# Seven block products in another order, and the work beside the heads planned anew: a hybrid recurrent layer on one core

## The chip, the cores and the metric

The kernel runs on one core of one Trainium2 chip. The metric is the device time of one execution in microseconds; for the kernel before it is the median of three runs.

## The reference, cut to what matters

One layer on 1024 tokens of width 1024, all in float32. The part that the change touches is the mixing layer: one wide projection of the normalised input, two recurrent branches, and their gates.

```
h = rmsnorm(x)
proj = h @ w_in               # q,k,v,z of 8 delta heads; q,k,v,r of 4 GLA heads; two merge gates
q_a, k_a, v_a = silu(conv4(...))          # branch A: gated delta rule, chunks of 64, 8 heads of 128
o_a = rmsnorm(gated_delta_rule(...)) * silu(z)
o_b = rmsnorm(gla(q_b, k_b, v_b, gate)) * silu(r)     # branch B: 4 heads, values of 256
merged = sigmoid(gate_a) * (o_a @ w_a) + sigmoid(gate_b) * (o_b @ w_b)
x = x + merged @ w_out
x = x + cross_attention(rmsnorm(x), rmsnorm(mem))
x = x + relu(rmsnorm(x) @ w1) ** 2 @ w2
return rmsnorm(x)
```

## The kernel before, in words

Float32 products are made of three TensorE passes (`mm3`, lines 584, 586 and 588): both operands are split into a rounded high part and a low remainder, and high by high, high by low and low by high are added in one PSUM tile. ScalarE makes the high part of a weight block (line 624, or 986 where the block is negated), VectorE the low part (625, 987).

The large projections are computed by a seven-product scheme for 2x2 blocks. A **unit** is one such projection of 256 columns. The seven products p0 to p6 take a sum of weight blocks A11, A12, A21, A22 and a fixed sum of input blocks each. In the trace the input block names the product: A0a is p0, A0b is p1, t2, t4 and t6 are p2, p4 and p6 (all three read "t" in the profile), A1b is p3 and A1a is p5. Each product is 12 matmuls of 512 columns. The products of a unit add into three PSUM banks (`BANK`): p0, p2, p4 and p6 all add to the first, p1 has the second alone, p3 and p5 share the third. After each product its bank is read once: p0, p3 and p2 are copied out by ScalarE (line 937), p1, p4 and p5 are added to the result by VectorE (942 to 946), p6 goes to an activation. The next product of the same bank adds to what stands there, so its first matmul waits until the bank has been read.

In the phase with the GLA heads (`phase_gla`, some 150 to 707 us in the profile) the weight sums are not formed by an engine. `gla_w` lets GpSimd issue four accumulating transfers per unit (line 972, `more`), each of which adds a 256 KB block from HBM to a block in SBUF. In a unit's program order they are: the **first sum** A21 += A22, at p0; the **second sum** A11 += A21, behind p0's split, used by p4; the **third sum** A21 += A11, behind p3's split, used by p2; the **fourth sum** A21 += A12, behind p2's split, used by p5. So p3 must come before p2 and p2 before p5. The split weights lie in a ring of four buffers ("wop", `RING`), the raw blocks in four ("raw"), which is two units.

The units of one GLA head are r, then k, q and v of two delta heads, then qk of the next GLA head. Beside them run the GLA head's own work (gates, scores, a scan of eight steps, norm, output), the short convolution (line 1316) and, in `phase_gdn` (some 707 to 1110 us), the delta heads: a forward substitution on VectorE (`gdn_subst`), an inverse by TensorE (lines 1490 and 1499), a scan per pair of heads, and dense units beside it (gates 5 to 15, z, and the folded attention weights Q and O).

Two things set the order of instructions. The program pushes the dense units as generators on a queue and takes a number of matmuls from it at each place (`fill`, with the constants FA to FJ, SFILL, PFILL, TFILL, and the lists EXTRA, FILL and LASTG). Then a planner (`Plan`) replays the traced program with a cost for each instruction and fixes the order on every engine; each engine runs its list in order. LAYP and LAYQ set the places of the delta heads' buffers in SBUF.

Of the kernel before, what the change touches and what calls it, by code (L numbers as in the profile page):

```python
# [37 lines left out]
DIRP, FW = (6,), 5  # L38
DXB = 6
EXB, THB, GLOV, TE = 5, 1, (0, 2, 4, 6), 1  # L40
FA, FB, FC, FD, FE, FG, FH, FI = 23, 31, 30, 28, 47, 24, 0, 0
SE = ((0, 0, 0, 0, 0, 0, 0, 0), (0, 1, 0, 1, 1, 1, 0, 1), (0, 1, 0, 1, 0, 1, 0, 0))
FJ = 24
KRAW = 4
LAYW = (("raw", 2048, 2), ("whi", 4096, 2), ("wlo", 4096, 2))
FF = ((24, 24), (24, 24))
# [11 lines left out]
def bcol(t, n):  # L58
# [5 lines left out]
           "Reciprocal", "StreamTranspose", "TensorScalarAffineSelect")  # L64
ENGINES = {mybir.EngineType.PE: "tensor", mybir.EngineType.DVE: "vector", mybir.EngineType.Activation: "scalar",
           mybir.EngineType.Pool: "gpsimd", mybir.EngineType.SP: "sync"}
EXTRA = (('v', 'k', 't', 'q'), ('v', 't', 'k', 'q'), ('k', 'v', 't', 'q'), ('k', 'v', 't', 'q'))
QB, FOLDB = 2, 1
SFILL, PFILL, TFILL = 4, (2, 12), (4, 14, 0, 10, 10, 6)
FILL = ((7, 'z6'), ('z0', 6, 10, 'Q2'), (9, 'O1', 'z5', 'z3', 'Q3', 'z1'), ('z2', 'z4', 'O0', 11, 'O3', 'z7', 8, 'Q1', 5), ('O2', 13, 'Q0', 12))  # L70
LASTG = (14, 15)
LAYP = (('PF', 8192, 1), ('pr', 1024, 1), ('NT1', 4096, 2), ('NT0', 4096, 2), ('Pm', 4096, 1), ('dm', 4096, 2), ('k0', 4096, 2), ('kdt0', 4096, 2), ('kdt1', 4096, 2), ('k1', 4096, 2), ('q', 4096, 2))
LAYQ = (('AT', 4096, 2), ('v0', 4096, 2), ('X', 4096, 2), ('sz', 2048, 2), ('v1', 4096, 2), ('acc', 2048, 2))
OUT = "out_0_dram"
HOLD, MARGIN = 0, 0
SOON = 0
# [12 lines left out]
class Op:  # L89
# [7 lines left out]
    def __init__(self, ins, flex):  # L97
        eng = self.eng = ENGINES[ins.engine]
        ins_, outs = [[x for x in q if getattr(x, "bass_ap", None) is not None] for q in (ins.ins, ins.outs)]
        n = size(outs[0])  # L100
        psum = lambda x: x.bass_ap.tensor.name[:3] in ("pd_", "ps_")
        self.name, self.opcode, self.acc = ins.name, ins.opcode, []
        for w, q in enumerate((ins_, outs)):
            for x in q:
                p = x.ap[0][0]
                lows, span = [x.bass_ap.offset % p if p > 1 else x.bass_ap.offset], 0
                for st, k in sorted(x.ap[1:]):
                    if st <= span + 1 or k * len(lows) > 16:
# [12 lines left out]
        times = {"vector": (150 + scan + n * 1.042 + 60 * scalar, 85, 34, 35), "gpsimd": (290 + n * 1.98 if sums else 160 + n * 0.9, 45, 60, 35)}  # L121
        if sums and n <= 16:
            times["gpsimd"] = 430 + n * 152, 45, 60, 35
        if ins.opcode == "TensorReduce":
            times["vector"] = 420, 85, 34, 35
        if ins.opcode == "StreamTranspose":
            times["vector"] = 1880 if far else 1245, 85, 34, 35
        if ins.opcode == "Memset" and far:
            times["gpsimd"] = 450, 45, 60, 35
        self.times = {e: (d - early, early + own, early + lat) for e, (d, early, own, lat) in times.items()}  # L130
        if ins.opcode == "DMACopy":
            self.dma, self.cost, self.own, self.lat = True, ISSUE, LAND, LAND
            self.bytes = n * 4 * outs[0].ap[0][1]
            if eng == "gpsimd":
                self.cost, self.bytes = 1200, 2 * self.bytes
            if ins_[0].bass_ap.tensor.name in HEADIN:
                self.bytes *= RATE / 390
        elif eng == "tensor":
            m = size(ins_[0])
            if ins.is_transpose:  # L140
                self.cost = m * 0.85
            elif ins_[0].dtype == F32R:
                self.cost = m * 0.4463 + (4 if m < HALF else 0)
            elif max(m, size(ins_[1])) == 64:
# [358 lines left out]
class Layer:  # L503
# [454 lines left out]

        return evict

    SUMS = (0, 1, 3, 2, 4, 5, 6)

    def gla_w(self):
# [8 lines left out]
        more = lambda dst, src: nc.gpsimd.dma_start(dst, src, accum_op=ADD)  # L972

        for p in self.SUMS:
            for o, (a, src) in zip(ops, bl):
                A11, A12, A21, A22 = a
                if p == 0:
                    more(A21, src[3])
                if A11.shape[-1] == P:
                    t = self.til(wp, [P, 2, n, P], "wop", F32R, bufs=RING)  # L980
                    o[p] = t[:, 0], t[:, 1]
                else:
                    o[p] = [self.til(wp, [P, n, 256], "wop", F32R, bufs=RING) for _ in range(2)]
                w, (hi, lo) = (A11, A12, A21, A21, A11, A21, A22)[p], o[p]
                if p in (2, 3, 6):
                    nc.scalar.activation(hi, w, AF.Copy, scale=-1.0)  # L986
                    nc.vector.scalar_tensor_tensor(lo, w, -1.0, hi.bitcast(F32), MUL, SUB)  # L987
                else:
                    self.split(w, hi, lo, nc.vector if p in GLOV else None)
                if p in (0, 2, 3):  # L990
                    more(*{0: (A11, src[2]), 3: (A21, src[0]), 2: (A21, src[1])}[p])
        return n, ops

    def gla_dense(self, evicts, after=None):

        n, ws = self.gla_w()
        yield
        bank = self.banks(2)
        for p in self.SUMS:
            if p == 2:  # L1000
                self.fetch_w()
            for i, (w, evict) in enumerate(zip(ws, evicts)):
# [11 lines left out]
                pt, new = bank(p, i)  # L1014
# [1503 lines left out]
```

## Time and profile before

| | before |
|---|---|
| median of three runs | 2169.34 us (2164.31 to 2181.07) |
| profiled execution | 2169.7 us |
| its span | 2167.8 us |
| TensorE (PE) busy | 2112.3 us, 97% |
| VectorE (DVE) busy | 1540.3 us, 71% |
| ScalarE (ACT) busy | 1208.5 us, 56% |
| GpSimd (POOL) busy | 229.3 us, 11% |
| mean granted TensorE clock | 0.995 |

The profiled execution is 0.4 us above the median, and 1.9 us of it lie outside the span. TensorE is busy nearly all the time, so only the time in which it waits, or runs at a lower clock, can be won by another order. GpSimd's busy time counts the issue of a transfer and not its flight.

### The profile page before, as it was taken

Reading aid. Unit: us, or ns where it says so; the run is one execution under the profiler, and the core shown is the slowest. Engines: PE = TensorE matmul, PEld = TensorE weight load, DVE = VectorE, ACT = ScalarE, POOL = GpSimd, SP = SyncE. Lnnn points to the kernel's source line nnn. Section 1 sums busy time; section 2 is a strip of 40 time slices with the busy share of each in tenths; the row PEclk is TensorE's granted clock in tenths of the full one; section 3 lists DMA queues with packets and bytes.
Section 4 is the critical chain, followed back from the end, with each engine's and each line's share of the span. In section 5 each row is a group of like instructions: output and inputs, shape, how many; then the busy total and the mean of one; then the engine's idle time right before and its main releaser. Section 6 shows DMA issues by size and latency. Waiting matters only on the chain. (4 is left out here: it accounts for less than half of the span.)

```text
span 2167.8 us, 31186 instructions
## 1 busy us (share of the span) xinstructions
PE 2112.3 (97%) x10938; PEld 1784.9 (82%) x10938; DVE 1540.3 (71%) x2744; ACT 1208.5 (56%) x2393; POOL 229.3 (11%) x260
## 2 busy tenths in 40 slices
PE   8999989999899999999999999999999999999998
PEld 8888767798677889889988888888788888888787
DVE  7846857636656678869558899659968667566755
ACT  7456746635645657586645455665755557443433
POOL 0112111111111423121100000000100000000000
PEclk9999999999999999999999999999999999999999
DMA  8554554644545634544487762325454456778742
GB/s 321 153 126 91 131 123 98 162 102 99 155 94 142 209 97 161 185 151 161 147 284 231 235 222 80 114 88 166 129 177 133 151 174 203 249 248 273 239 158 102
DMA packets 171613, 355.81 MB, mean 164 GB/s; under 512 B 18488, under 2 KB 27192, under 8 KB 171456
## 3 DMA queue, kind: packets, MB, share of 16 engines
q1 hardware_dynamic: 158064, 327.57, 45.5%
q0 software_dynamic: 13248, 26.22, 7.7%
q8 instruction: 86, 1.41, 0.3%
q14 instruction: 71, 0.58, 0.1%
q10 hardware_dynamic: 144, 0.03, 0.0%
HBM read 253.57 MB, written 100.17 MB: 163 GB/s over the span
## 5 line engine op out<-in xcount | busy, mean ns | idle before, releaser
L624 ACT ACTIVATE wop<-raw 128x512 fp32r<-128x512 f32 (+1 forms) x451 | 291.5, 651 | 362.1 <-PE pd L588 157.5
L625 DVE TENSOR_TENSOR wop<-raw,wop 128x512 fp32r<-128x512 f32 (+1 forms) x428 | 298.9, 702 | 231.8 <-ACT wop L624 226.2
L584 PE MATMUL pd<-t,wop 128*128 128x512 f32 x332 | 133.6, 402 | 19.4 <-ACT wop L986 10.4
L588 PE MATMUL pd<-t,wop 128*128 128x512 f32 x332 | 132.1, 398 | 0.9 <-DVE wop L987 0.9
L586 PE MATMUL pd<-t,wop 128*128 128x512 f32 x332 | 131.6, 396 | 0.0
L584 PE MATMUL pd<-A1b,wop 128*128 128x512 f32 x272 | 106.4, 392 | 0.0
L586 PE MATMUL pd<-A1b,wop 128*128 128x512 f32 x272 | 106.1, 390 | 0.0
L588 PE MATMUL pd<-A1b,wop 128*128 128x512 f32 x260 | 101.3, 391 | 1.6 <-DVE wop L987 1.6
L584 PEld LDWEIGHTS pd<-t,wop 128*128 128x128 f32 x332 | 63.2, 190 | 41.2 <-ACT wop L986 13.3
L1316 DVE SCALAR_TENSOR_TENSOR dx<-dx,convw,dx 128x1023 f32<-128x1023 f32 (+2 forms) x72 | 91.0, 1288 | 7.5 <-ACT dx L1314 6.8
L987 DVE SCALAR_TENSOR_TENSOR wop<-raw,wop 128x512 fp32r<-128x512 f32 (+1 forms) x69 | 50.8, 736 | 58.3 <-ACT wop L986 58.1
L986 ACT ACTIVATE wop<-raw 128x512 fp32r<-128x512 f32 (+1 forms) x69 | 45.8, 664 | 79.3 <-PE pd L588 29.9
L584 PE MATMUL pd<-A1a,wop 128*128 128x512 f32 x208 | 82.0, 394 | 3.7 <-ACT wop L624 3.5
L586 PE MATMUL pd<-A1a,wop 128*128 128x512 f32 x208 | 81.1, 390 | 0.0
L588 PEld LDWEIGHTS pd<-t,wop 128*128 128x128 f32 x332 | 63.4, 191 | 16.7 <-DVE wop L987 3.4
L588 PE MATMUL pd<-A1a,wop 128*128 128x512 f32 x196 | 76.9, 393 | 0.0
L586 PEld LDWEIGHTS pd<-t,wop 128*128 128x128 f32 x332 | 63.2, 190 | 12.4
L624 ACT ACTIVATE whi<-raw 128x512 fp32r<-128x512 f32 x70 | 43.2, 628 | 41.6 <-PE pd L586 28.1
L584 PEld LDWEIGHTS pd<-A1b,wop 128*128 128x128 f32 x272 | 51.1, 188 | 10.6 <-ACT wop L624 0.3
L586 PEld LDWEIGHTS pd<-A1b,wop 128*128 128x128 f32 x272 | 51.1, 188 | 10.3
L588 PEld LDWEIGHTS pd<-A1b,wop 128*128 128x128 f32 x260 | 48.8, 188 | 12.0 <-DVE wop L987 2.0
L625 DVE TENSOR_TENSOR wlo<-raw,whi 128x512 fp32r<-128x512 f32 x64 | 43.6, 685 | 16.1 <-ACT whi L624 15.8
(654 smaller groups left out, 6587.9 us busy)
## 6 DMA issues: line engine op xcount, KB each, us to landing
raw<-in_w_dram SPq DMA_DIRECT2D x120, 256.0 KB, 4.1
raw<-in_w_dram SPq DMA_DIRECT2D x32, 512.0 KB, 3.8
e<-ad SPq DMA_DIRECT2D x63, 256.0 KB, 4.8
ad<-q SPq DMA_DIRECT2D x45, 256.0 KB, 2.8
rawa<-ad SPq DMA_DIRECT2D x42, 256.0 KB, 4.6
A0b<-tgd SPq DMA_DIRECT2D x32, 256.0 KB, 4.5
ad<-acc SPq DMA_DIRECT2D x30, 256.0 KB, 2.3
ad<-u SPq DMA_DIRECT2D x30, 256.0 KB, 2.8
```

Source lines behind the costliest of these rows:

```text
L584: nc.tensor.matmul(out, lh, rh, start=first and i == 0, stop=False, skip_group_check=True)
L586: nc.tensor.matmul(out, lh, rl, start=False, stop=False, skip_group_check=True)
L588: nc.tensor.matmul(out, ll, rh, start=False, stop=last and i == n - 1, skip_group_check=True)
L624: nc.scalar.activation(hi, raw, AF.Copy)
L625: (lo_eng or nc.gpsimd).tensor_tensor(lo, raw, hi.bitcast(F32), SUB)
L986: nc.scalar.activation(hi, w, AF.Copy, scale=-1.0)
L987: nc.vector.scalar_tensor_tensor(lo, w, -1.0, hi.bitcast(F32), MUL, SUB)
L1316: self.nc.vector.scalar_tensor_tensor(y[:, d:], x[:, :T - d], cw[:, 3 - d:4 - d], y[:, d:], MUL, ADD)
```

## The change

The seven products of a unit get one of two orders. Units with one result tile set run p0, p3, p2, p1, p4, p5, p6, so that two neighbours never add to the same PSUM bank. The first unit (two evictions) and the two v units of the GLA heads (a list of two) keep the order of before, p0, p1, p3, p2, p4, p5, p6. The next unit's raw blocks are fetched at the fourth product, as before. The accumulating transfers stay, with their program order in `gla_w` following the products.

Beside that the numbers that place the work change: fewer matmuls are taken behind the scores (FC) and behind the next gate (FD), one at each step of the GLA scan (FH, none before), EXTRA puts k first in the first head and v first in the other three, the dense units of the delta heads are dealt out in another way (gate 14 comes in earlier and gate 5 later), and two SBUF layouts are permuted. The planner takes 900 ns, not 1200, for GpSimd's issue of a transfer.

```
-FA, FB, FC, FD, FE, FG, FH, FI = 23, 31, 30, 28, 47, 24, 0, 0
+FA, FB, FC, FD, FE, FG, FH, FI = 23, 31, 22, 20, 46, 24, 1, 0
-FJ = 24
+FJ = 12
-EXTRA = (('v', 'k', 't', 'q'), ('v', 't', 'k', 'q'), ('k', 'v', 't', 'q'), ('k', 'v', 't', 'q'))
+EXTRA = (('k', 'v', 't', 'q'), ('v', 't', 'k', 'q'), ('v', 't', 'k', 'q'), ('v', 't', 'k', 'q'))
-SFILL, PFILL, TFILL = 4, (2, 12), (4, 14, 0, 10, 10, 6)
+SFILL, PFILL, TFILL = 3, (6, 12), (4, 14, 0, 8, 14, 10)
-FILL = ((7, 'z6'), ('z0', 6, 10, 'Q2'), ...
+FILL = ((7,), ('z0', 6, 10, 'z6', 'Q2'), ...
-LASTG = (14, 15)
+LASTG = (15, 5)
...
-                self.cost, self.bytes = 1200, 2 * self.bytes
+                self.cost, self.bytes = 900, 2 * self.bytes
...
-    SUMS = (0, 1, 3, 2, 4, 5, 6)
+    SUMS = ((0, 3, 2, 1, 4, 5, 6), (0, 1, 3, 2, 4, 5, 6))
...
-        for p in self.SUMS:
+        for p in order:
...
-        n, ws = self.gla_w()
+        order = self.SUMS[len(evicts) > 1 or isinstance(evicts[0], list)]
+        n, ws = self.gla_w(order)
...
-        for p in self.SUMS:
-            if p == 2:
+        for i, p in enumerate(order):
+            if i == 3:
                 self.fetch_w()
```

What the planner makes of it is shown at three places. First TensorE, at the second delta unit of the first head (k before, v after): the first matmul of each of its seven products. pd names the PSUM tile, the next name is the input block. Before:

```order
L584 MATMUL pd_330_2514<-A0a_10_202,wop_323_2490 128x512
L584 MATMUL pd_332_2529<-A0b_11_203,wop_324_2494 128x512
L584 MATMUL pd_333_2543<-A1b_163_1270,wop_325_2497 128x512
L584 MATMUL pd_330_2514<-t2_152_1157,wop_326_2501 128x512
L584 MATMUL pd_330_2514<-t4_153_1158,wop_327_2505 128x512
L584 MATMUL pd_333_2543<-A1a_12_204,wop_328_2508 128x512
L584 MATMUL pd_330_2514<-t6_154_1159,wop_329_2511 128x512
```

The same engine and place in the change:

```order
L584 MATMUL pd_330_2518<-A0a_10_202,wop_323_2494 128x512
L584 MATMUL pd_332_2533<-A1b_163_1270,wop_324_2498 128x512
L584 MATMUL pd_330_2518<-t2_152_1157,wop_325_2502 128x512
L584 MATMUL pd_336_2565<-A0b_11_203,wop_326_2506 128x512
L584 MATMUL pd_330_2518<-t4_153_1158,wop_327_2509 128x512
L584 MATMUL pd_332_2533<-A1a_12_204,wop_328_2512 128x512
L584 MATMUL pd_330_2518<-t6_154_1159,wop_329_2515 128x512
```

p2 (t2) moved from the fourth to the third place, one product sooner, and p1 (A0b) now stands between p2 and p4 (t4), which add to one bank.

Second GpSimd's list, where the qk unit of the second head follows the q unit: the sums of qk and the first sum of the r unit behind it. Before:

```order
L972 DMA raw_355_2729<-in_w_lqk_dram 128x512 [waits DVE_49]
L972 DMA raw_369_2870<-in_w_lr_dram 128x512 [waits DMAHW1_49,DMASW4_49,DMASW1_49]
L972 DMA raw_355_2729<-in_w_lqk_dram 128x512 [waits DMASW3_49,DVE_49]
L972 DMA raw_355_2729<-in_w_lqk_dram 128x512 [waits DMASW7_49,DVE_49]
L972 DMA raw_369_2870<-in_w_lr_dram 128x512 [waits DVE_49]
```

In the change:

```order
L972 DMA raw_354_2728<-in_w_lqk_dram 128x512 [waits DVE_49]
L972 DMA raw_354_2728<-in_w_lqk_dram 128x512 [waits DMASW3_49,DVE_49]
L972 DMA raw_368_2869<-in_w_lr_dram 128x512 [waits DMAHW0_49,DMASW4_49,DMASW1_49]
L972 DMA raw_354_2728<-in_w_lqk_dram 128x512 [waits DMASW6_49,DVE_49]
L972 DMA raw_368_2869<-in_w_lr_dram 128x512 [waits DVE_49]
```

The first row is qk's second sum, and the row that waits for a hardware transfer (DMAHW) is r's first sum. It stood between qk's second and third sums and stands now between the third and the fourth.

Third ScalarE's list at the same second delta unit. L937 copies p0's bank out, L986 makes p2's high part. Before:

```order
L1314 ACTIVATE dx_322_2482<-dx_318_2417,convw_6_194 128x1024
L937 ACTIVATE dx_331_2527<-pd_330_2514 128x512
L1084 ACT_TABLE_LOAD
L1084 ACTIVATE dx_321_2462<-dx_321_2462 128x512
L986 ACTIVATE wop_326_2501<-raw_319_2419 128x512
L624 ACTIVATE wop_327_2505<-raw_319_2419 128x512
```

In the change:

```order
L1078 ACTIVATE dx_317_2403<-pd_308_2338 128x512
L1315 ACTIVATE dx_322_2484<-dx_317_2403,convw_6_194 128x1024
L986 ACTIVATE wop_325_2502<-raw_318_2418 128x512
L624 ACTIVATE wop_326_2506<-raw_319_2419 128x512
L937 ACTIVATE dx_331_2531<-pd_330_2518 128x512
```

The copy of p0's bank stood ahead of p2's split and stands now behind it and behind p1's split.

More of the change, by code (lines that the diff above doesn't have):

```diff
@@ L66 @@
            mybir.EngineType.Pool: "gpsimd", mybir.EngineType.SP: "sync"}
-EXTRA = (('v', 'k', 't', 'q'), ('v', 't', 'k', 'q'), ('k', 'v', 't', 'q'), ('k', 'v', 't', 'q'))
+EXTRA = (('k', 'v', 't', 'q'), ('v', 't', 'k', 'q'), ('v', 't', 'k', 'q'), ('v', 't', 'k', 'q'))
 QB, FOLDB = 2, 1
-SFILL, PFILL, TFILL = 4, (2, 12), (4, 14, 0, 10, 10, 6)
-FILL = ((7, 'z6'), ('z0', 6, 10, 'Q2'), (9, 'O1', 'z5', 'z3', 'Q3', 'z1'), ('z2', 'z4', 'O0', 11, 'O3', 'z7', 8, 'Q1', 5), ('O2', 13, 'Q0', 12))
-LASTG = (14, 15)
-LAYP = (('PF', 8192, 1), ('pr', 1024, 1), ('NT1', 4096, 2), ('NT0', 4096, 2), ('Pm', 4096, 1), ('dm', 4096, 2), ('k0', 4096, 2), ('kdt0', 4096, 2), ('kdt1', 4096, 2), ('k1', 4096, 2), ('q', 4096, 2))
-LAYQ = (('AT', 4096, 2), ('v0', 4096, 2), ('X', 4096, 2), ('sz', 2048, 2), ('v1', 4096, 2), ('acc', 2048, 2))
+SFILL, PFILL, TFILL = 3, (6, 12), (4, 14, 0, 8, 14, 10)
+FILL = ((7,), ('z0', 6, 10, 'z6', 'Q2'), (9, 14, 'O1', 'z5', 'z1'), ('z2', 'z4', 'z3', 'O0', 11, 13, 'O3', 'Q0', 'Q1'), ('Q3', 'z7', 'O2', 12, 8))
+LASTG = (15, 5)
+LAYP = (('PF', 8192, 1), ('k1', 4096, 2), ('NT1', 4096, 2), ('NT0', 4096, 2), ('Pm', 4096, 1), ('dm', 4096, 2), ('k0', 4096, 2), ('kdt0', 4096, 2), ('kdt1', 4096, 2), ('pr', 1024, 1), ('q', 4096, 2))
+LAYQ = (('AT', 4096, 2), ('v0', 4096, 2), ('acc', 2048, 2), ('sz', 2048, 2), ('v1', 4096, 2), ('X', 4096, 2))
 OUT = "out_0_dram"
@@ L959, in joined, with gla_w @@
         return evict
-    SUMS = (0, 1, 3, 2, 4, 5, 6)
-    def gla_w(self):
+    SUMS = ((0, 3, 2, 1, 4, 5, 6), (0, 1, 3, 2, 4, 5, 6))
+    def gla_w(self, order):
         nc, wp = self.nc, self.wp
@@ L994, in gla_dense @@
     def gla_dense(self, evicts, after=None):
-        n, ws = self.gla_w()
+        order = self.SUMS[len(evicts) > 1 or isinstance(evicts[0], list)]
+        n, ws = self.gla_w(order)
         yield
         bank = self.banks(2)
-        for p in self.SUMS:
-            if p == 2:
+        for i, p in enumerate(order):
+            if i == 3:
                 self.fetch_w()
-            for i, (w, evict) in enumerate(zip(ws, evicts)):
+            for u, (w, evict) in enumerate(zip(ws, evicts)):
                 x, (hi, lo) = self.bs[p], w[p]
@@ L1013, in gla_dense @@
                     continue
-                pt, new = bank(p, i)
+                pt, new = bank(p, u)
                 yield from self.mm3(pt, [((hi[:, k], lo[:, k]), (x[:, 0, k], x[:, 1, k])) for k in range(n)], new, p in (1, 5, 6))
```

## The prediction

> **What bounds the kernel now.** The page's first part is read first: who is busy, and for how much of the span.
>
> ```profile
> PE 2112.3 (97%) x10938; PEld 1784.9 (82%) x10938; DVE 1540.3 (71%) x2744; ACT 1208.5 (56%) x2393; POOL 229.3 (11%) x260
> ```
>
> TensorE (PE) is busy for 2112.3 of 2167.8 us. The change removes no matmul, so at most the other 55.5 us, and what is lost to a lower clock, can be won. Next comes the table of busy time by stretches: the phase with the GLA heads, the delta heads, and what follows (length, then busy time with count of PE, PEld, DVE, ACT and POOL, the granted clock, the DMA share, GB/s).
>
> ```profile
> 150.00:707.00 557.00, 524.64 (x2766) 434.44 (x2765) 362.53 (x511) 306.13 (x494) 91.94 (x108) 0.99 0.50 119
> 707.00:1110.00 403.00, 398.17 (x2644) 355.86 (x2642) 305.63 (x756) 260.71 (x750) 93.78 (x115) 0.99 0.50 165
> 1110.00:2167.80 1057.80, 1045.76 (x4684) 865.36 (x4682) 769.59 (x1321) 557.09 (x1007) 28.28 (x18) 1.00 0.55 181
> ```
>
> PE stands idle for 557.00 - 524.64 = 32.4 us in the GLA phase, 4.8 in the delta phase and 12.0 in all that follows, which is twice as long. The GLA phase is where the change works. What it waits for there, in the table of waits (waiting line, what it waited for, us in total, times, longest):
>
> ```profile
> PE pd L584 <- ACT wop L986: 10.9, 7, 2.9
> PE pd L584 <- ACT dx L937: 6.6, 9, 2.2
> PE pd L584 <- ACT wop L624: 4.9, 6, 1.3
> PE pd L588 <- DVE wop L987: 2.4, 2, 1.6
> PE pd L584 <- ACT qk L937: 2.1, 3, 0.7
> PE pd L586 <- DVE wop L625: 1.1, 1, 1.1
> PE pd L586 <- DVE wop L987: 1.0, 2, 0.8
> PE pd L584 <- DVE qk L946: 0.5, 1, 0.5
> ```
>
> There are two families. L937 and L946 read a bank out: PE waits to add to a bank that the product before it has just filled. These **bank waits** are 6.6 + 2.1 + 0.5 = 9.2 us in 13 places. The others wait for split weights (**weight waits**): 10.9 + 2.4 + 1.0 = 14.3 us on L986 and L987 (the negated blocks of p3 and p2, mostly p2's, which needs the third sum) and 4.9 + 1.1 = 6.0 on L624 and L625; 20.3 together.
>
> **The bank waits.** One of them from near, on PE's timeline (start, us, instruction, idle before it and what ended it), at p2 and then p4:
>
> ```profile
> 385.33 0.39 PE L586 MATMUL pd<-t,wop 128*128 128x512 f32 x1
> 385.55 0.39 PE L588 MATMUL pd<-t,wop 128*128 128x512 f32 x1
> 386.63 0.50 PE L584 MATMUL pd<-t,wop 128*128 128x512 f32 x1 [0.69 <-ACT dx L937]
> ```
>
> Matmuls start every 0.22 to 0.23 us, so a product of 12 takes 2.7 us. The first of p4 starts 1.08 us after the last of p2, 0.85 more than the pace, where the idle column says 0.69. The thirteen places cost 9.2 + 13 x 0.16 = 11.3 us. With p1 between p2 and p4 the copy has 2.7 us to happen in, and needs this:
>
> ```profile
> L937 ACT ACTIVATE dx<-pd x51: 576/598/604, 107.5 to 694.4; 128x512 f32<-128x512 f32 x51
> ```
>
> 0.6 us. So the waits behind p2 go whole, -11.3, unless ScalarE's list puts the copy late. It does that elsewhere: the order of the change shows p0's copy behind p2's split, and p2 adds to p0's bank. By the whole list that is so in 7 of 20 units, against 3 before. There p2's first matmul waits for the split, which it needs anyway, then for p1's split and the copy, each about 0.6 us: 1.2 us, but only where the third sum comes late. I take three such cases, 3 x 1.1 = +3.3. **Bank waits: -8** (bounds -11.3 and -11.3 + 7 x 1.2 = -3).
>
> **The weight waits.** For a sum one reads GpSimd's rows beside those of the engines that use it. At the second q unit (p3's split; then on GpSimd its second sum, a foreign first sum of qk, its third sum; then p2's split and p2's first matmul):
>
> ```profile
> 556.22 0.69 DVE L987 SCALAR_TENSOR_TENSOR wop<-raw,wop 128x512 fp32r<-128x512 f32 x1
> ...
> 553.13 0.89 POOL L972 DMA_DIRECT2D raw<-in_w_gq_dram  x1 [8.05 <-DVE wop L625]
> 558.55 0.88 POOL L972 DMA_DIRECT2D raw<-in_w_lqk_dram  x1 [4.53 <-issue]
> 562.64 0.88 POOL L972 DMA_DIRECT2D raw<-in_w_gq_dram  x1 [3.22 <-DVE dx L1316]
> ...
> 566.90 0.63 ACT L986 ACTIVATE wop<-raw 128x512 fp32r<-128x512 f32 x1 [2.40 <-DMA raw<-in_w_gq_dram]
> ...
> 567.58 0.49 PE L584 MATMUL pd<-t,wop 128*128 128x512 f32 x1 [1.44 <-ACT wop L986]
> ```
>
> The split at 556.22 (p3's) released the third sum, but that was issued at 562.64, because the second sum was in flight from 553.13 and another unit's first sum stood between. One accumulating transfer follows another: the issues lie 5.42 and 4.09 us apart, as far as one takes to land.
>
> ```profile
> DMA to landing us min/median/max: 3.6/4.1/6.7
> ```
>
> So place in GpSimd's list decides, and a transfer costs its unit 4.1 us. In the change that foreign sum stands between the third and the fourth (the second place shown above) at this unit, and likewise at two others whose p2 waits are these:
>
> ```profile
> 298.00 0.50 PE L584 MATMUL pd<-t,wop 128*128 128x512 f32 x1 [2.87 <-ACT wop L986]
> 614.97 0.50 PE L584 MATMUL pd<-t,wop 128*128 128x512 f32 x1 [2.87 <-ACT wop L986]
> ```
>
> There the third sum comes 4.1 us sooner, and p2 is wanted 2.7 us sooner, so 1.4 us is won: 2.87 becomes 1.5 twice and 1.44 goes, -4.2. The fourth sum waits for p2's split, one product sooner before p5 than until now: 2.7 us, more than any of L624's six waits (longest 1.3), so their 4.9 go. Against that, p2 comes one product sooner in every unit that has the new order. Those that waited for L986 or L987 anyway would pay up to 2.7 us each: seven at most, 19 us. The lower bound is nothing, if the split before, now also a product sooner, brings its sum sooner. Since most units of before show no p2 wait I stay near nothing, at +2. **Weight waits: -7** (bounds -20.3 and -9 + 19 = +10).
>
> **The clock.** The stretches with a granted clock of 0.50:
>
> ```profile
> 299.70:303.10 3.40, 2.85 (x7) 1.66 (x6) 0.00 (x0) 0.81 (x2) 0.25 (x1) 0.50 0.90 207
> 381.60:385.00 3.40, 3.02 (x7) 2.46 (x8) 3.08 (x5) 1.61 (x2) 0.88 (x1) 0.50 0.87 286
> 569.40:572.80 3.40, 3.40 (x12) 2.81 (x11) 0.00 (x0) 2.12 (x5) 0.14 (x1) 0.50 0.72 152
> 787.80:794.60 6.80, 6.17 (x29) 6.18 (x30) 1.20 (x3) 5.52 (x10) 1.95 (x6) 0.50 0.25 77
> ```
>
> Each follows a wait: 2.87 us before 298.00, 1.44 before 567.58, a p2 wait at 380.39 and, in the delta phase, this:
>
> ```profile
> PE ps L1490 <- ACT PF L1478: 2.6, 1, 2.6
> PE ps L1542 <- ACT dl L1537: 0.9, 1, 0.9
> ```
>
> At half rate a stretch loses half its length: 3 x 1.7 + 3.4 = 8.5 us. The windows fall where waits happen to lie, so with fewer waits I take half: **-4** (bounds -8.5, and +7 should four more appear).
>
> The Trainium skill bears on this in "TensorE: Matmul & The Clock Gate", section "Part 1: The HAM clock gate (the "warmup" mystery)": it says that the clock drops to half after at least one idle window of about 3.4 us. The rows here disagree: the waits ahead of these stretches are 2.9 us and shorter, so the measurement decides. By the page's rule no wait of this kernel would cost clock, this term would be 0 and the sum 4 us less of a gain, 2154.
>
> **The delta phase and the rest.** Between the first gram products and the inverse at L1490 stands dense work that covers the substitution. Counted in the two lists at the pace of the rows above, it grows from 55 to about 59 us, which is past the 55 + 2.6 that the substitution took. But each scan step now gets three matmuls, not four (SFILL), so the 0.9 us wait may come back several times. Of 3.5 us I take **-1** (bounds -3.5 and, if each of the last scan's eight steps waits 0.9, +7). The planner's 900 ns and the layouts add no work; behind 1110 us the code is the same, and its largest wait is this:
>
> ```profile
> PE pd L584 <- ACT q L937: 1.7, 1, 1.7
> ```
>
> That stage gets 0.
>
> **Sum.** -8 - 7 - 4 - 1 = -20 us. Against the profiled execution's 2169.7 (span 2167.8 and 1.9 outside), that gives **2150**, 0.9% less. The profiled execution lies 0.4 us above the median of 2169.34, so no correction is made.
>
> **Rivals.** *All weight waits go too.* If the earlier place of p2's and p3's splits pulls the sums along, the terms are -11.3, -20.3, -8.5 and -3.5: -43.6, so **2126**. For it: the ring has a free buffer one product sooner. Against it: the sums follow each other at 4.1 us and more whatever the splits do.
>
> *The chain of sums takes the gain back.* A unit needs first, second and third sum in a row before p2, and that is as long as before while PE arrives 2.7 us sooner. Seven times 2.7 is +19, with -11.3 for the banks, -4 for the clock and the p5 waits partly back: about +3, **2172**. For it: the 2.40 us in which ScalarE waited for the sum at 566.90, so the chain is without slack there. Against it: most units show none.
>
> *Slower: a foreign first sum ahead of a unit's own second.* The third rival is told by these rows, of GpSimd and then PE:
>
> ```profile
> 361.08 0.88 POOL L972 DMA_DIRECT2D raw<-in_w_gq_dram  x1 [12.27 <-DMA raw<-in_w_gq_dram]
> 365.47 0.88 POOL L972 DMA_DIRECT2D raw<-in_w_gk_dram  x1 [3.51 <-DVE dx L944]
> ...
> 374.85 0.50 PE L588 MATMUL pd<-A1b,wop 128*128 128x512 f32 x1 [1.57 <-DVE wop L987]
> 380.39 0.50 PE L584 MATMUL pd<-t,wop 128*128 128x512 f32 x1 [1.20 <-ACT wop L986]
> ```
>
> At 361.08 GpSimd waited for q's raw block, 12.27 us, with k's second sum (365.47) queued behind; k's p3 and p2 waited afterwards. Before, the list has this at one k unit and one v unit. In the change it stands so at the second unit of each of four heads. If the raw block is late each time, the unit loses one transfer's landing and one sum, 4.1 + 4.4 = 8.5 us: 4 x 8.5 = 34, with four more halved windows +7, less the bank's 11.3: +30, **2199**. It decides as soon as the raw load lands later than p0's split. Against it: with 12.27 us of waiting, only 1.57 and 1.20 reached PE.
>
> That the change does nothing is excluded for the order: PE's rows above show p1 between p2 and p4.
>
> **How the numbers follow.** Forecast 0.48, all weight waits go 0.16, the chain takes it back 0.20, slower 0.16. The forecast's own range, with each term about half way to its bounds (4, 7, 6 and 3 us, which make 10 to 12 when added as squares), is 2138 to 2162. A change of under 1% (21.7 us, so 2148 to 2191) is about what a measurement of this kernel can't tell from none. Faster: 0.16 and some two fifths of the forecast's 0.48, 0.36. Slower: 0.16 and a little of the chain's case, 0.18. The rest, 0.46, is within 1%. The range must leave out no more than 0.2: from 2126, which leaves out half of the fastest case, to 2186, which leaves out most of the slowest.
>
> **What will show it.** In the GLA phase the waits of L584 for dx and qk of L937 should fall from 8.7 us to 2 to 4, all of them now at p2 and none at p4; L624's 4.9 should be gone; L986 and L987 should keep 9 to 13. There should be one or two halved windows, and L1490's wait under 1 us. The forecast is wrong if GpSimd's rows show waits for raw blocks ahead of a second sum that PE pays in full (slower), if p2 waits 2 us or more in over six units (no change), or if p2 waits nowhere (faster).

## The result: no difference, and the profile after

The changed kernel takes 2170.34 us, median of 20 runs; the kernel before takes 2167.34 us over 20 runs beside it. The ratio is 1.0013, 95% interval 1.0000 to 1.0026. The forecast was 2150 us, 0.9% faster. The time is inside the range given, but no gain came. The profiled execution after took 2173.8 us, with a span of 2172.1 us against 2167.8 before.

First the busy times on the page of the changed kernel, then its stretches (the same columns as before, same bounds):

```profile
PE 2115.9 (97%) x10938; PEld 1791.6 (82%) x10938; DVE 1543.5 (71%) x2740; ACT 1211.6 (56%) x2395; POOL 231.3 (11%) x264
```

```profile
150.00:707.00 557.00, 523.93 (x2739) 438.80 (x2738) 355.96 (x507) 301.58 (x491) 90.23 (x106) 0.97 0.49 118
707.00:1110.00 403.00, 396.13 (x2629) 351.87 (x2628) 312.16 (x753) 262.27 (x751) 96.29 (x120) 1.00 0.50 162
```

TensorE (PE) stands idle for 33.1 us in the GLA phase, where it stood idle for 32.4 before; and its granted clock there fell from 0.99 to 0.97. So the waits were exchanged and not removed, and the clock was lost on top. The table of PE's waits between 150 and 707 us says what was exchanged for what (waiting line, what it waited for, us, times, longest):

```profile
PE pd L584 <- ACT wop L986: 13.6, 9, 2.5
PE ps L656 <- ACT dx L1085: 5.5, 3, 2.3
PE ps L1187 <- DVE S L1193: 4.8, 1, 4.8
PE pd L584 <- ACT dx L937: 4.6, 2, 2.8
PE pd L584 <- DVE v L942: 1.5, 1, 1.5
PE pd L586 <- DVE wop L625: 1.0, 1, 1.0
PE pd L584 <- ACT wop L624: 0.6, 1, 0.6
```

Gone are the bank waits at p4 and p6 (none is left there), which were nearly all of the 9.2 us, and 4.3 of the 4.9 us on L624 (p5's weights in five of its six places, p0's in the sixth). New are 2.7 us more for p2's weights (L986), 4.6 us for p0's bank copy (L937, now at p2), 4.6 us more for the transposes behind the short convolution (L656) and 4.8 us in the GLA scan (L1187). In the delta phase the wait at L1490 (L1491 after) went, as forecast, and others came:

```profile
PE ps L1428 <- DMA q<-gdq: 1.6, 1, 1.6
PE pd L588 <- DVE wlo L625: 1.5, 3, 0.6
...
PE ps L1491 <- ACT PF L1479: 0.3, 1, 0.3
```

Now one unit from near, the r unit whose p2 waited for 2.87 us before and was to win. VectorE's row is p3's split; GpSimd's rows are the unit's second sum, its third, and a foreign first sum; then p2's split and p2:

```profile
603.46 0.68 DVE L987 SCALAR_TENSOR_TENSOR wop<-raw,wop 128x512 fp32r<-128x512 f32 x1
...
603.34 0.88 POOL L972 DMA_DIRECT2D raw<-in_w_lr_dram  x1 [6.59 <-DVE wop L625]
609.70 0.88 POOL L972 DMA_DIRECT2D raw<-in_w_lr_dram  x1 [5.48 <-issue]
613.95 0.87 POOL L972 DMA_DIRECT2D raw<-in_w_gv_dram  x1 [3.37 <-DMA raw<-in_w_lr_dram]
...
613.72 0.63 ACT L986 ACTIVATE wop<-raw 128x512 fp32r<-128x512 f32 x1 [3.30 <-DMA raw<-in_w_lr_dram]
...
614.40 0.50 PE L584 MATMUL pd<-t,wop 128*128 128x512 f32 x1 [1.90 <-ACT wop L986]
```

The foreign sum does stand behind the third now, and p2's wait fell from 2.87 to 1.90 us, where 1.5 was forecast. But p3's split was done at 604.1 and the third sum was issued at 609.70: the unit's **own second sum**, which nobody needs before p4, was in flight in between. It is ready first, since p0's split comes before p3's, and so it stands ahead of the third in every unit, before and after. The prediction took the foreign sum for the obstacle and counted the own one as fixed.

### The profile page after: what moved, and what is told of

Its sections match the earlier page's. It is cut to its first block, busy times and chain, and to the rows that moved or that the text cites. A ratio compares the mean times of both kernels' runs of the same rounds, so it can differ in the third digit from the quotient of the medians.

```text
span 2172.1 us, 31150 instructions
## 1 busy us (share of the span) xinstructions
PE 2115.9 (97%) x10938; PEld 1791.6 (82%) x10938; DVE 1543.5 (71%) x2740; ACT 1211.6 (56%) x2395; POOL 231.3 (11%) x264
## 5 line engine op out<-in xcount | busy, mean ns | idle before, releaser
L624 ACT ACTIVATE wop<-raw 128x512 fp32r<-128x512 f32 (+1 forms) x451 | 291.3, 652 | 371.7 <-PE pd L588 156.2
L584 PE MATMUL pd<-t,wop 128*128 128x512 f32 x332 | 135.7, 409 | 16.7 <-ACT wop L986 12.0
L588 PE MATMUL pd<-t,wop 128*128 128x512 f32 x332 | 135.1, 407 | 0.5 <-DVE wop L987 0.5
L586 PE MATMUL pd<-t,wop 128*128 128x512 f32 x332 | 134.5, 405 | 0.0
L987 DVE SCALAR_TENSOR_TENSOR wop<-raw,wop 128x512 fp32r<-128x512 f32 (+1 forms) x69 | 50.6, 734 | 61.2 <-ACT wop L986 61.0
L986 ACT ACTIVATE wop<-raw 128x512 fp32r<-128x512 f32 (+1 forms) x69 | 45.8, 663 | 78.2 <-PE pd L588 23.0
L624 ACT ACTIVATE whi<-raw 128x512 fp32r<-128x512 f32 x70 | 43.0, 626 | 35.6 <-PE pd L586 16.6
```

What stands on the lines that cost most here:

```text
L584: nc.tensor.matmul(out, lh, rh, start=first and i == 0, stop=False, skip_group_check=True)
L586: nc.tensor.matmul(out, lh, rl, start=False, stop=False, skip_group_check=True)
L588: nc.tensor.matmul(out, ll, rh, start=False, stop=last and i == n - 1, skip_group_check=True)
L624: nc.scalar.activation(hi, raw, AF.Copy)
```

## The experiments

Each time is a median of 4 to 10 runs taken beside the kernel before; the ratio and its 95% interval are to that. "Numbers" are the constants of the change (fills, EXTRA, the delta phase's lists, layouts, 900 ns).

**One half of the change at a time.** First the new product order with every number of before (in short, the names alone):

```
-EXTRA, FA .. FJ, SFILL .. LASTG, LAYP, LAYQ, 900     (of the change)
+EXTRA, FA .. FJ, SFILL .. LASTG, LAYP, LAYQ, 1200    (of before)
```

> The new order of the seven products alone, with every number of before (fills, EXTRA, layouts, 1200 ns). Theory A (the chain of sums takes the gain back): the 13 bank waits are gone (11 us), p2's waits for L986 and L987 grow to 20 to 28 us in the GLA phase and the clock costs some us more than before, so 2162 to 2178 us, no change. Theory B (the order gains what was forecast and the new numbers lose it again): 2145 to 2153 us, with p2's waits at 13 us or less. Theory C (the sums are not what holds p2; its split waits for a free buffer of the ring): the same time as A, but ScalarE's rows ahead of p2's split end on a matmul and not on a transfer.

Measured 2179.75 us, ratio 1.0066 (1.0049 to 1.0083): slower than before by more than theory A allowed. The waits are not those of theory A either: L986 and L987 hold 13.2 us and not 20 to 28, while p0's copy holds 9.6 (7.0 of it in one wait at p2) and the scan at L1187 10.1. Theory C falls, since ScalarE's longest waits ahead of L986 end on transfers (5.2 and 6.1 us). Then the numbers with the old order:

```
-    SUMS = ((0, 3, 2, 1, 4, 5, 6), (0, 1, 3, 2, 4, 5, 6))
+    SUMS = ((0, 1, 3, 2, 4, 5, 6), (0, 1, 3, 2, 4, 5, 6))
```

> All the new numbers, with the product order of before in every unit. Theory A: the bank waits are back (9 to 11 us), p2's waits for its split are back at 10 to 15 us, and the waits that came with the numbers stay (4.8 us in the GLA scan, about 5 us of the conv's transposes); 2165 to 2182 us. Theory B (the numbers lose 15 to 20 us): 2182 us or more.

Measured 2190.46 us, 1.0119 (1.0104 to 1.0134), in theory B's range, but B's other half (the order alone gains) had just failed. Either half alone loses, 14.6 and 25.3 us against the kernel before beside it; together they come back to nothing. The numbers fit this order, and gain little more than what the order loses. Theory B falls.

**The GLA fills of before, in the change.**

```
-FA, FB, FC, FD, FE, FG, FH, FI = 23, 31, 22, 20, 46, 24, 1, 0
-FJ = 12
+FA, FB, FC, FD, FE, FG, FH, FI = 23, 31, 30, 28, 47, 24, 0, 0
+FJ = 24
```

> The change with the numbers of matmuls taken in the GLA phase (FC 30, FD 28, FE 47, FH 0, FJ 24) as before. Theory A says that the fills explain only their own waits: the 4.8 us in the scan at L1187 and the halved clock behind it (3.4 us) go, p2's waits stay over 20 us; 2160 to 2168 us. Theory B (the fills are what lost the gain): 2150 us or less, with p2's waits under 13 us.

Measured 2175.1 us, 1.0052 (1.0032 to 1.0072), 0.4% above the change's ratio, so the new fills are not what lost the gain; the scan's waits did not go but doubled (10.2 us in two, now at L1185).

**What holds p2.** The exchange of second and third sum, written in the program's order:

```
-                if p in (0, 2, 3):
-                    more(*{0: (A11, src[2]), 3: (A21, src[0]), 2: (A21, src[1])}[p])
+                if p in (2, 3):
+                    more(A21, src[{3: 0, 2: 1}[p]])
+                if p == 3:
+                    more(A11, src[2])
```

> The change with the second and third sum of a unit exchanged: A21 += A11 is issued behind p3's split and A11 += A21 after it, so p2's block waits for two transfers and not three; p4, which needs the other one, comes two products later. Nothing is left out. Theory A (three transfers one after another hold p2): one transfer, 4 to 5 us, leaves p2's chain, p2's waits fall from about 26 us to under 10, half of the low clock goes with them (7 us), and the time is 2145 to 2155 us. Theory C (p3's split or the ring holds p2): p2's waits stay within 5 us of those of the change, 2165 to 2175 us. If the exchange only moves the wait to p4, waits of L584 for L624 appear there and the time is within 1% of the change.

Measured 2173.92 us, 1.0041 (1.0025 to 1.0057). It tells nothing of theory A: in the trace a unit's next sum was still issued right behind p0's split, several times before p3's split was done, so it was the second as before. The planner sorts by what is ready. So, on top of that edit, the start order was put into the plan, with one entry in `sums` per unit: the second sum may start only after the third.

```
...
+        for x in sums:
+            first[x[2]].add(x[1])
```

> In the run before, the exchange of second and third sum did not reach GpSimd's list: the planner issues what is ready first, and p0's split comes before p3's. Here the planner must start a unit's third sum ahead of its second (a start order in the plan, nothing else). Theory A (the unit's own second sum stands in front of the third): p2's splits come about 4 us sooner in every unit, PE's gaps before p2 fall from 20 us to under 6, half of the low clock goes, 2148 to 2158 us. Theory D (GpSimd's queue is full, so whatever is put last is waited for): the wait moves to p4 and p5 (L624, over 8 us) and the time stays within 8 us of the change. Theory E (the foreign first sums are what holds p2): only the units without a foreign sum ahead gain, the four second units and the v-to-k ones keep 2 to 3 us each, 2158 to 2166 us.

Measured 2173.84 us, 1.0033 (1.0017 to 1.0049). PE's waits in the GLA phase (lines 7 and more higher here: 631 is 624, 993 is 986, 994 is 987, 663 is 656, 944 is 937):

```profile
PE ps L663 <- ACT dx L1094: 9.5, 5, 3.2
PE pd L591 <- ACT wop L631: 5.0, 3, 2.6
PE ps L1196 <- DVE S L1200: 2.0, 2, 1.6
PE pd L591 <- ACT dx L944: 1.8, 3, 1.2
...
PE pd L591 <- ACT wop L993: 0.4, 1, 0.4
```

The wait for p2's split fell from 13.6 to 0.4 us: that the own second sum held p2 is shown. L631 (p5's and p4's weights) rose from 0.6 to 5.0, the way theory D said but not to its 8, and the convolution's transposes from 5.5 to 9.5. Even so PE's gaps in the GLA phase fell by 8 us and the time lost to half rate there from 17 to 5 us, so that the phase ends 18 us sooner than in the change. Behind it 15 us went again: PE's gaps in the delta phase (start to start over the pace) rose from 8 to 16 us, and half rate came back there (3.4 us). So the GLA phase gained and the whole did not. The exchange with the delta phase's numbers of before was not run. Keeping the next unit's first sum behind this unit's second as well:

```
+        for x, y in zip(sums, sums[1:]):
+            first[y[0]].add(x[2])
```

> The same, and the next unit's first sum may start only after this unit's second, so no foreign sum stands ahead of a unit's own second or third. Theory A and E together: all of p2's gaps under 3 us, 2142 to 2154 us, better than the run above by the 8 to 12 us of the four second units if E holds and by nothing if the forced exchange had taken them already. Theory D: the next unit's p3 waits for its first sum (L986 and L987 at A1b) and the time is no better than the run above.

Measured 2196.18 us, 1.0120 (1.0096 to 1.0143): worse by 22 us. The waits went to p0's copies (11.5 us), to L624 (7.4) and to the scan (6.7). The third rival's place is no lever by itself.

**The planner told of the chain.**

```
-                self.cost, self.bytes = 900, 2 * self.bytes
+                self.cost, self.bytes = 4200, 2 * self.bytes
```

> The change with 4200 ns, not 900, for GpSimd's issue of a transfer in the planner, about what one takes to land on the chip; the kernel's work is the same. If the planner's blindness to the chain of transfers is what lets p2 come ahead of its sum, PE gets other work there, p2's gaps fall to under 10 us and the time to 2150 to 2162 us. If the order on GpSimd alone decides, the gaps stay at 15 to 22 us and the time within 8 us of the change.

Measured 2219.14 us, 1.0228 (1.0209 to 1.0246), a plain miss. PE's waits in the GLA phase:

```profile
PE pd L584 <- ACT wop L986: 27.0, 9, 6.4
PE pd L584 <- ACT wop L624: 6.3, 4, 3.0
PE pd L586 <- DVE wop L987: 4.6, 3, 3.0
```

A truer cost gave a worse plan; why was not tried.

**Fewer transfers.** The first sum needs nothing from HBM, since both its blocks lie in SBUF. In the change:

```
-                    more(A21, src[3])
+                    nc.vector.tensor_tensor(A21, A21, A22, ADD)
```

> The change with the first sum A21 += A22 done by VectorE in SBUF (one tensor_tensor of 128x512 per unit; both blocks are there) in place of an accumulating transfer. Three transfers per unit are left, and no foreign first sum waits for a raw block in GpSimd's list. Theory E: the gaps of the four second units go and those of the units with the own second sum ahead stay: 2155 to 2164 us. Theory D (a full queue): a quarter of the queue's load goes, all gaps of p2 fall by half or more, 2150 us or less. Against both: 20 additions on VectorE, 0.7 to 1 us each, come between its splits; if these hold PE up, 2170 us or more.

Measured 2150.6 us, 0.9906 (0.9883 to 0.9930). (The planner put two of the 23 additions on GpSimd, 1.7 us each, and 21 on VectorE.) Three transfers per unit instead of four give the gain that the order was to bring:

```profile
PE ps L656 <- ACT dx L1085: 7.0, 6, 2.2
PE pd L584 <- ACT wop L986: 3.4, 3, 1.7
PE pd L584 <- ACT dx L937: 2.4, 2, 1.7
```

The same edit in the other three combinations of order and numbers tells what the order is worth when the sums have room:

> The new numbers and the first sum on VectorE, with the products in the old order in every unit: against the same with the new order (2150.6 us) it gives the worth of the order alone once the sums' chain has room. Theory A: the bank waits are back at p4 (13 places, 9 to 11 us, some half-clock windows), so 2160 to 2168 us. If the order is worth nothing even then, 2147 to 2155 us. If the numbers only fit the new order, as the 20 us between the two without VectorE's sum suggest, 2170 us or more.

Measured 2162.62 us, 0.9976 (0.9965 to 0.9987), in theory A's range, and the bank waits are back (9.7 us for dx and 2.1 for qk at L937). But they are not where the 12 us lie. The GLA phase ends only 2.8 us later than with the new order (677.4 against 674.6 us); in the delta phase PE's idle time is 19 us against 13, and half rate takes 8.5 us against 3.4. Theory A's number came by luck.

> The kernel before with nothing changed but the first sum, done by VectorE. If the relief of GpSimd's chain is what made 2150.6 us and the change of order and numbers has no part in it, 2145 to 2153 us. If the gain needs the new order (Theory A: the old one still pays its bank waits, 11 us, while its p2 waits of 13 us shrink to about 5), 2155 to 2163 us.

Measured 2140.92 us, 0.9869 (0.9855 to 0.9884): better than either expectation, with the old order, the old numbers and 11 us of bank waits still in place:

```profile
PE pd L584 <- ACT dx L937: 9.1, 10, 4.1
PE pd L588 <- DVE wop L987: 2.2, 2, 1.4
PE pd L584 <- ACT qk L937: 2.2, 3, 0.8
PE pd L584 <- ACT wop L986: 1.2, 1, 1.2
```

> The new order with the numbers of before and the first sum on VectorE. Theory A: against the order alone (2179.8 us, 12 to 15 us above before) p2's gaps of 22 us fall below 10, 2158 to 2168 us. If the order gains wherever the chain has room and the numbers don't matter, 2148 to 2156 us.

Measured 2149.06 us, 0.9905 (0.9891 to 0.9920): 8 us slower than with the old order.

The fourth sum can be done in SBUF too:

```
+                if p == 2:
+                    nc.vector.tensor_tensor(A21, A21, A12, ADD)
-                if p in (0, 2, 3):
+                if p in (0, 3):
```

> The change with the first and the fourth sum on VectorE, so two transfers per unit are left. Theory D (the queue's load counts): p2's gaps fall below 3 us and the time to 2140 to 2147 us. Theory A (only what stands ahead of the third sum counts, and the fourth stands behind it): within 4 us of the run with the first sum alone, 2147 to 2155 us; VectorE's 20 further additions may cost some of it.

Measured 2147.12 us, 0.9897 (0.9880 to 0.9913), on the border between D and A; the GLA phase has no half-clock window left, the delta phase has three in a row.

**The delta phase's numbers.** Alone, in the kernel before:

> The kernel before with only the numbers of the delta phase changed (SFILL, PFILL, TFILL, FILL, LASTG and the two layouts); order, GLA fills and sums as before. If these numbers lose time by themselves, the delta phase's gaps grow from 5 us to 13 or more and the time is 2175 to 2190 us. If they lose only beside the new GLA numbers, 2160 to 2172 us.

Measured 2169.9 us, 1.0012 (0.9996 to 1.0029): no difference. Put back in the change with both sums on VectorE:

> The change with first and fourth sum on VectorE and the delta phase's numbers of before; new order, new GLA numbers. The GLA phase should keep its 17 us of gaps without a halved window, and the delta phase fall from 13 us of gaps and 5 us of clock to 5 and 3: 2130 to 2140 us. If the delta numbers of before fit only what stood ahead of them before, 2145 us or more.

Measured 2131.89 us, 0.9828 (0.9803 to 0.9853), 15 us better than with the new ones. So they lose only beside what the GLA phase leaves behind it.

**Both sums on VectorE, numbers of before, old and new order.**

> The kernel before with first and fourth sum on VectorE; old order, old numbers. 13 bank waits stay (9 to 12 us), all weight waits in the GLA phase under 5 us: 2134 to 2142 us, at most 6 us better than with the first sum alone (2140.9).

Measured **2126.66 us, 0.9800 (0.9775 to 0.9826)**: the best of all, 2.0% under the kernel before, and better than expected. The page and PE's waits in the GLA phase:

```profile
PE 2098.1 (99%) x10938; PEld 1782.5 (84%) x10938; DVE 1579.2 (74%) x2791; ACT 1218.3 (57%) x2399; POOL 193.6 (9%) x213
```

```profile
PE pd L584 <- ACT dx L937: 2.2, 1, 2.2
PE pd L584 <- DVE dx L944: 2.2, 1, 2.2
PE pd L588 <- DVE wop L987: 1.5, 3, 0.8
PE pd L586 <- DVE wop L987: 1.0, 1, 1.0
```

All but two of the bank waits are gone (4.4 us are left), and that with the old order, in which p4 follows p2. PE's timeline shows how (A1a is p5):

```profile
390.95 0.39 PE L588 MATMUL pd<-t,wop 128*128 128x512 f32 x1
391.18 0.39 PE L584 MATMUL pd<-A1a,wop 128*128 128x512 f32 x1
391.40 0.39 PE L586 MATMUL pd<-A1a,wop 128*128 128x512 f32 x1
391.63 0.39 PE L588 MATMUL pd<-A1a,wop 128*128 128x512 f32 x1
391.86 0.39 PE L584 MATMUL pd<-A1a,wop 128*128 128x512 f32 x1
392.08 0.45 PE L584 MATMUL pd<-t,wop 128*128 128x512 f32 x1
```

With p5's weights ready in time the planner puts four of p5's matmuls between p2 and p4, 0.9 us, which is what the bank's copy takes. Such a piece of p5 stands there in 15 of 19 units, against 7 in the kernel before and 8 with the first sum alone on VectorE, so it is the fourth sum that makes it possible. The price is 43 additions on VectorE (0.68 us each, 1.22 for the four of twice the width) and three that the planner put on GpSimd.

> The same two sums on VectorE with the new order and the numbers of before. If bank waits were all that separates the orders once the sums have room, 8 to 12 us less than the run above, 2124 to 2132 us. If p0's copy behind the splits, the scan's waits (L1185, L1187) and the conv's transposes take their place, as they did with the first sum alone (2149.1 against 2140.9), the same or up to 10 us more than the run above.

Measured 2143.19 us, 0.9876 (0.9853 to 0.9899): 17 us slower than the old order, the second expectation and more. One wait stands out there:

```profile
PE pd L584 <- ACT dx L937: 9.8, 3, 7.3
```

It is p2 of the third delta unit of the first head, waiting for p0's copy, which ScalarE's list has behind convolution, exponentials and table loads. So p0's copy was moved to VectorE:

```
+            elif p == 0:
+                nc.vector.tensor_scalar(dest(*b), pt, scale, None, MUL)
```

> New order, numbers of before, first and fourth sum on VectorE, and p0's bank copied out by VectorE in place of ScalarE. If the copy's place in ScalarE's list is what the new order loses by, the 9.8 us of waits for L937 at p2 and the half-clock window behind them go: 2125 to 2134 us. If the copy on VectorE waits as long behind its splits, or another wait takes over, 2138 us or more.

Measured 2146.25 us, 0.9901 (0.9884 to 0.9917). That one wait went; p2's split (5.7 us), the copies on VectorE (5.7) and the transposes (4.5) took its place. The copy is not the cause by itself.

Last, the fourth sum alone in the kernel before:

> The kernel before with only the fourth sum (p5's) on VectorE. If p5's weights, ready in time, let the planner put four of p5's matmuls between p2 and p4 and so cover the bank wait, the bank waits fall from 13 to 3 or fewer places, p2's weight waits stay at 10 us or more: 2145 to 2155 us. If the bank waits go only with both sums, they stay at 9 us or more and the time is 2158 to 2168 us.

Measured 2148.87 us, 0.9911 (0.9897 to 0.9926), in the time of the first theory, though L986 came down too. Pieces of p5 stand between p2 and p4 in 16 of 19 units, and bank waits there are left in few places. But a wait of the same kind as above, 8.6 us for p0's copy, stands here with the **old** order, so that jam on ScalarE is not the new order's alone:

```profile
PE pd L584 <- ACT dx L937: 11.0, 4, 8.6
PE pd L584 <- ACT wop L986: 4.9, 5, 2.4
```

The medians side by side (us; the kernel before was between 2165 and 2169 each time):

| sums of a unit by transfer | old order, old numbers | new order, old numbers | old order, new numbers | new order, new numbers |
|---|---|---|---|---|
| four | 2167.3 | 2179.8 | 2190.5 | 2170.3 |
| three (first on VectorE) | 2140.9 | 2149.1 | 2162.6 | 2150.6 |
| two (first and fourth) | 2126.7 | 2143.2 | not run | 2147.1 |

The traces tell in which phase each difference lies. The GLA phase ends with the last matmul on the units' split weights (wop), up to which every trace has the same 3599 matmuls. In the kernel before, in the change and in the change with the forced exchange:

```profile
702.65 0.39 PE L588 MATMUL pd<-t,wop 128*128 128x512 f32 x1
...
707.48 0.39 PE L588 MATMUL pd<-t,wop 128*128 128x512 f32 x1
...
689.48 0.39 PE L595 MATMUL pd<-t,wop 128*128 128x512 f32 x1
```

One profiled execution each, in us:

| run | GLA phase ends | rest of the span |
|---|---|---|
| before | 703.0 | 1464.8 |
| the change | 707.9 | 1464.2 |
| new order, old numbers | 715.3 | 1462.9 |
| old order, new numbers | 705.6 | 1483.1 |
| the change, exchange forced | 689.9 | 1479.6 |
| first sum on VectorE: old order, old numbers | 679.0 | 1460.3 |
| the same: new order, old numbers | 684.1 | 1464.2 |
| the same: new order, new numbers | 674.6 | 1474.4 |
| the same: old order, new numbers | 677.4 | 1488.2 |
| first and fourth: old order, old numbers | 668.2 | 1457.3 |
| the same: new order, old numbers | 679.8 | 1461.0 |
| the same: new order, new numbers | 670.8 | 1475.5 |
| the same, with the old delta numbers | 670.8 | 1458.1 |

So the change loses its 4 us in the GLA phase. With the delta numbers of before the rest takes 1457 to 1465 us in all nine runs that have them; with the new ones it takes 1462 to 1488 us in the eleven others, and the gains of the GLA phase are partly lost there. The last two rows differ in these numbers alone, and by 17 us.

## Why the prediction was wrong, point by point

**Bank waits, -8.** The mechanism was right and its size nearly: no wait stands between p2 and p4 any more, and 4.6 us of waits for p0's copy at p2 came instead, where +3.3 was taken. Moving p2 nearer to p0 moved the tight pair from p2 and p4 to p0 and p2. At both places ScalarE had first waited 4.8 and 4.2 us for the third sum, to make p2's split, which its list has ahead of the copy.

**Weight waits, -7.** This is the step that failed, in its smallest term. The three units with a foreign sum went from 7.2 to 3.7 us, -3.5 where -4.2 was forecast. L624 went from 4.9 to 0.6, as said, though one of its six waits before, 1.3 us, was p0's and not p5's. For all the other units the prediction took +2, because few of them showed a wait. There p2's waits for its split grew from 5.5 to 11.1 us, +5.6, and with the 4.6 us for the copies behind late splits it is +10. The prediction saw the unit's own second sum ahead of its third, took it as fixed and put no price on it for these units. The forced exchange showed the price: with that sum out of the way the waits on L986 and L987 fall from 14.9 to 2.2 us and the GLA phase ends 18 us sooner.

The second rival (the chain of sums takes the gain back, 2172 us, chance 0.20) named the right chain, and its time is within 2 us, but that is in part luck. It had +19 for p2 and -4 for the clock; p2 took 7 us more (with the copies), the clock 9, and 9 came from the scan and the convolution, which it did not have. The sign given for it, p2 waiting 2 us or more in over six units, did not come either: by the idle column three units did.

**The clock, -4.** Wrong in sign, and the largest miss. Seven stretches at half rate stand in the GLA phase of the profiled execution, three of them double, where three single ones stood before: 17 us lost against 5. The double one of the delta phase went (-3.4), so the term is +9. The sum of the waits is the same, but they are fewer and longer (20 against 35), or two stand near each other. The forced exchange has three single stretches there again, 5 us.

**Scan and convolution, 0.** The 4.8 us at L1187 and the 4.6 us more at L656, 9.4 together, were in no term. Fewer matmuls taken behind the scores (FC) and one at each scan step (FH) were read in the diff and not priced; yet the old fills in the change did not remove the scan's wait but doubled it, so a price for these constants alone would not have been right.

**Delta phase, -1.** The wait at L1490 went, as forecast, with the half-clock window behind it, and as much came back in small waits (4.7 us of waits before, 6.8 after). Alone these numbers are worth nothing.

**Third rival (foreign first sum), +30.** In the change the foreign sums do stand ahead of a unit's second sum at the second delta units, and p2 waits there 1.8 to 2.8 us, not 8.5. In the forced exchange they still stand there in all four heads, and yet p2's splits are hardly waited for, so it was not the foreign sum that held p2. Removing them with the start order cost 22 us more. With the first sum done by VectorE, which takes them away altogether, the change gains 20 us; how much of that is the foreign place and how much the shorter chain, these runs do not separate.

What stays open is why the new order loses with the numbers of before, by 14.6 us against the kernel before beside it and by 8 and 17 us in the other two rows of the first table. By the second table most of it, 12, 5 and 12 us, lies in the GLA phase; with the GLA numbers of the change and two sums on VectorE the new order costs 2.6 us there (670.8 against 668.2). It is not the bank wait, since that is gone; not the sums alone, since it stays with two transfers; not p0's copy alone. Each edit makes the planner arrange every engine anew, and differences of 10 us between two plans of equal work were seen for which no single cause was found.

## What to carry to other kernels

When a wait disappears between two steps, ask what the next step is fed by, and follow that queue in the order in which it is served: here four transfers in a row per unit, of which the one that was needed stood behind one that could wait. A gain in one phase can be lost in the next, so look at where each phase ends and not only at the total. A bank wait of 0.9 us needs no new product order if some other ready work can be put into it, and making that work ready early gained more than reordering. Constants that were found for one arrangement belong to it: either half alone lost 14 us and more.

## What the runs showed of the hardware that was not expected

The clock follows the busy time of fixed stretches of 3.41 us. In the changed kernel (length, then busy time of PE and the rest; the granted clock is the third figure from the end), pairs of such a stretch and the one behind it:

```profile
543.60:547.01 3.41, 1.48 (x5) 0.78 (x5) 1.56 (x3) 2.16 (x4) 0.42 (x1) 1.00 0.13 22
547.01:553.84 6.83, 5.34 (x20) 4.67 (x21) 5.67 (x12) 4.84 (x9) 0.46 (x1) 0.50 0.60 177
611.87:615.28 3.41, 1.51 (x6) 0.64 (x5) 0.90 (x2) 1.56 (x3) 0.87 (x1) 1.00 0.29 52
615.28:618.69 3.41, 3.41 (x9) 2.64 (x10) 0.99 (x2) 0.59 (x2) 0.47 (x1) 0.50 0.53 77
243.23:246.64 3.41, 1.83 (x9) 1.17 (x7) 0.00 (x0) 0.43 (x1) 0.00 (x0) 1.00 0.54 77
246.64:250.05 3.41, 2.16 (x9) 1.80 (x10) 3.18 (x5) 3.39 (x6) 0.88 (x1) 1.00 0.17 11
```

The stretches with PE busy for 1.48 and 1.51 us were followed by half rate, the one with 1.83 us was not. Over the 20 traces of this case, stretches that ran at full rate themselves, and away from a program's two ends, were always followed by half rate where PE was busy for under 1.5 us (65 stretches). Between 1.5 and 1.93 us it went either way (26 halved, 52 not), and above that none was followed by half rate, with one exception: in the run with p0's copy on VectorE a stretch in which PE was busy throughout, with matmuls of 64 columns, was followed by half rate at 857.5 us. So the stretch need not be idle throughout, and 2 us of waiting within one were enough. The Trainium skill, in "TensorE: Matmul & The Clock Gate", section "Part 1: The HAM clock gate (the "warmup" mystery)", gives the same free-running window and asks for an idle one; the length agrees, the condition does not. By these counts two waits of 1 us in one stretch cost 1.7 us more (half of the next stretch), and the same two in different stretches nothing.

Accumulating transfers from GpSimd were served one at a time in every trace: the next was never issued before the last had landed, whichever unit they belong to. In the kernel before, 20 issues for which the profile shows no other wait came 0.31 us behind the landing of the one ahead. In the changed kernel one took 3.7 to 8.4 us from issue to landing, with a median of 4.1. An addition of the same block on VectorE took 0.68 us.
